# Moving the seven-product units of a feed-forward layer one place ahead among the up groups

## The chip, the cores and the metric

The kernel runs on one core of one Trainium2 chip. The metric is the device time of one execution in microseconds (us), the lower the better. Several executions were timed, and one more was recorded by the hardware profiler. Engines are called by their usual short names: PE is TensorE (matrix products), DVE is VectorE, ACT is ScalarE, POOL is GpSimd, SP is SyncE, which here only starts transfers.

## The reference

The program is a trunk of two encoder layers over 256 positions of width 2048, in float32. Each layer has a mixer (layer 0: pooling and attention, layer 1: a bidirectional mLSTM) and then a gated feed-forward block. Only the feed-forward block is touched by the change:

```python
D_MODEL, SEQ, D_FF, CONV_WIDTH = 2048, 256, 5632, 3

def conv_ffn(x, w_up, conv_w, conv_b, w_down):
    u = x @ w_up                                   # (256, 2048) @ (2048, 11264)
    up = jnp.pad(u, ((0, 0), (1, 1), (0, 0)))
    c = conv_w.astype(u.dtype)
    u = c[0] * up[:, :-2] + c[1] * up[:, 1:-1] + c[2] * up[:, 2:] + conv_b.astype(u.dtype)
    gate, val = jnp.split(u, 2, axis=-1)
    return (jax.nn.silu(gate) * val) @ w_down      # (256, 5632) @ (5632, 2048)

def reference(...):
    for layer in range(2):
        x = x + mixer(layer, rms_norm(x, norm_mix[layer]))
        x = x + conv_ffn(rms_norm(x, norm_ffn[layer]), w_up[layer], conv_w[layer], conv_b[layer], w_down[layer])
    return x
```

## The kernel before

Every float32 operand of a product is split into a high and a low part, and a product is made of three matrix products of the parts (high by high, high by low, low by high). Weights come from memory as tiles of 128 x 1024 numbers (512 KB). `Stream` loads them on SP's queue in the order in which PE will use them (`load`, up to five tiles ahead), and splits each (`split`): ACT makes the high part (L127) and DVE the low part (L128) of a tile called `hl`. Splits are written two tiles ahead of their use, and there are four `hl` buffers.

The inner width of 5632 is made of 44 row tiles of 128, in six chunks of 4, 8, 8, 8, 8 and 8 (`FCH`). For each row tile there is one **up group** (`up`, L980): 64 matrix products that take four weight tiles, and behind them a chain of small steps that makes the gated value. In order: ACT copies half of the sums (L427), DVE adds (L428) and scales (L984), six ACT steps make the convolution's three terms (L989 to L991), DVE adds them (L992, L993), ACT applies SiLU (L997), DVE multiplies gate by value (L998, tile `silu`, written `s` in the profile), and ACT (L999) and DVE (L1000) split that into the tile `g`.

The down projection is done in two ways. Some of it is a plain product (`down`, `down_two`; the last chunk and, in layer 0, half the columns of chunk 1; written `dn`). The rest takes two row tiles (a *pair* `j`) and 1024 columns (a *half* `h`) as a 2 x 2 matrix of blocks and multiplies with **seven block products in place of eight**. They are made in two passes, A with four products for each pair and B with three, since an A pass fills all four of PSUM's `ps` tiles (written `pp` in the profile). A piece of a pass in the order of work is a **unit** (`unit`, L1023): `("A", c, h, js)` is pass A of chunk `c`, half `h`, for the pairs `js`. A chunk of eight row tiles has four pairs, and a pass is two units, for pairs 0 and 1 and for pairs 2 and 3. Here a unit is written A c/h:js, such as A 3/1:01.

The products need sums of blocks on both sides:

- sums of the activations are made by `combine` (L1002, called a **mix**, one for each pair), out of the four `s` quarters of two row tiles: three DVE steps (L1006 to L1008) and then a split of the results by ACT (L1012) and DVE (L1013) into the tiles `s3` (384 wide, read by pass A) and `s1` (128 wide, read by pass B). Both are called `s` in the profile; the widths tell them apart;
- sums of the weights are, for half 1, made while they are loaded: a transfer with addition for one tile (`Sum`, started on POOL) and two DVE additions of half a tile each for the next (`Chain`, L123 and L124). For half 0 they were made long before by other transfers (`Made`).

When a pass is done, `drain` adds its PSUM tiles to `acc` or to `x` on DVE (L1068; the first time some by ACT). After the last unit of a half, `total` makes eight more DVE steps (L1085).

PE runs in the order in which the program is written. The order of the other engines is chosen when the program is built: of the steps that are ready there, the one written first. Which unit stands behind which up group is written out by `_ffn_plan` (L1232): behind each up group of chunk `c` it puts at most one place of work of chunk `c - 1`, counted from the first up group of chunk `c`. `_ffn_weights` lays out the weights in the same order. A mix stands behind the units of its place:

```python
        for i in range(n):
            seq.append(("up", c, i))
            seq += slots[i] if i < len(slots) else []
            if c < len(FCH) - 1:
                seq += [("mix", c, j) for j in range(n // 2) if i == max(2 * j + 1, busy.get(j, 0))]
```

The last up group of the second layer and of the first is number 43; behind it come its unit, then `down_two` (two blocks of 512 columns together, first with row tiles 0 to 5 of the last chunk, then with 6 and 7), and `down` for the other two blocks.

## Time and profile before

| what | value |
|---|---|
| median of 3 timed runs | 2163.98 us (2162.7 to 2164.5) |
| profiled execution: its own time, and the span from its first to its last instruction | 2163.78 us, 2162.0 us |
| PE busy with products, share of the span | 2156.2 us, 100% |
| DVE busy | 1734.7 us, 80% |
| ACT busy | 1414.3 us, 65% |
| POOL busy | 212.7 us, 10% |
| moved by transfers | 555.29 MB, mean 257 GB/s |

A row of the timeline gives the start in us from the span's start, the busy time, the engine, the line of the kernel, the operation, what is written and read (`out<-in`), the shape and the count; a bracket at its end gives the idle time of the engine before it and what ended that. In the table of waits, a row names who waited for whom, and then gives the us in total, the number of times and the longest wait. Granted clock is the share of full speed that PE was allowed.

### The profile page before, as it was taken

What the parts mean: (1) busy time and instruction counts of PE and PEld (TensorE: products, weight loads), DVE (VectorE), ACT (ScalarE), POOL (GpSimd) and SP (SyncE); (2) the same over time, 40 slices, a digit from 0 to 9 for tenths busy, and PEclk for the clock granted to TensorE, in tenths of its full rate; (3) what the DMA queues carried; (4) which work ended last, traced back from release to release, by engine and by line L of the source; (5) the groups of instructions that cost most, each with busy time, mean ns of one, the idle gap of its engine ahead of it and who ended that gap; (6) DMA issues with size and microseconds to landing.
All of it is one profiled execution on the core that took longest, in us unless ns stands there. A gap on an engine that the chain in (4) does not pass through costs nothing.

```text
span 2162.0 us, 31902 instructions
## 1 busy us (share of the span) xinstructions
PE 2156.2 (100%) x11412; PEld 1844.2 (85%) x11412; DVE 1734.7 (80%) x2425; ACT 1414.3 (65%) x2208; POOL 212.7 (10%) x268
## 2 busy tenths in 40 slices
PE   9999999999999999999999999999999999999999
PEld 7888888888888888889888888888888888888887
DVE  7686688887988988986777676667889898988896
ACT  7665578766777767666454544457777777776763
POOL 0022111110100100001111111211100000000000
PEclk9999999999999999999999999999999999999999
DMA  9668989898999877779888888898978787887774
GB/s 323 213 202 250 287 250 311 248 280 247 298 296 293 287 257 232 266 232 252 231 246 251 237 250 230 273 276 249 289 226 285 258 283 246 265 262 251 233 249 162
DMA packets 164097, 555.29 MB, mean 257 GB/s; under 512 B 20602, under 2 KB 23202, under 8 KB 163938
## 3 DMA queue, kind: packets, MB, share of 16 engines
q1 hardware_dynamic: 129632, 462.88, 62.0%
q0 software_dynamic: 20704, 52.71, 14.8%
q10 hardware_dynamic: 13602, 37.67, 5.7%
q8 instruction: 89, 1.46, 0.3%
q14 instruction: 70, 0.57, 0.1%
HBM read 551.04 MB, written 69.25 MB: 287 GB/s over the span
## 4 chain that ended last, share of the span: by engine, by line
PE 97%; DVE 2%; DMA 1%; issue 0%; ACT 0%; DVEq 0%
PE up L264 44%; PE pp L264 15%; PE op L264 8%; PE dn L264 5%; PE mv L264 4%; PE mq L264 4%; PE mk L264 4%; PE mo L264 4%; PE qproj L264 3%; PE kproj L264 1%; PE vproj L264 1%; PE pool L264 1%; DVE hl L128 1%; PE qk L264 1%; PE av L264 1%; PE end L264 1%
## 5 line engine op out<-in xcount | busy, mean ns | idle before, releaser
L128 DVE TENSOR_TENSOR hl<-w,hl 128x1024 fp32r<-128x1024 f32 (+2 forms) x840 | 1009.4, 1214 | 218.4 <-ACT hl L127 216.0
L127 ACT CAST hl<-w 128x1024 fp32r<-128x1024 f32 (+2 forms) x839 | 863.4, 1047 | 451.4 <-PE up L264 145.3
L264 PE MATMUL up<-xx,hl 128*128 128x512 f32 (+1 forms) x5632 | 994.0, 337 | 0.0
L264 PEld LDWEIGHTS up<-xx,hl 128*128 128x128 f32 x5632 | 866.9, 188 | 130.9 <-DVE hl L128 0.5
L264 PE MATMUL pp<-hl,s 128*128 128x512 f32 x816 | 204.9, 392 | 0.3 <-DVE hl L128 0.3
L264 PEld LDWEIGHTS pp<-hl,s 128*128 128x128 f32 x816 | 150.4, 188 | 32.0 <-DVE hl L128 1.2
L473 POOL DMA_DIRECT2D m<-m x128 | 102.1, 800 | 701.0 <-PE up L264 293.1
L264 PE MATMUL pp<-hl,g 128*128 128x512 f32 x612 | 156.9, 391 | 0.0
L427 ACT COPY tb_up<-up 128x512 f32<-128x512 f32 x88 | 51.6, 587 | 123.4 <-PE up L264 123.2
L264 PEld LDWEIGHTS pp<-hl,g 128*128 128x128 f32 x612 | 112.2, 188 | 22.3
L991 ACT ACTIVATE y<-tb_up,conv 128x256 f32<-128x256 f32 x176 | 104.4, 593 | 0.0
L992 DVE TENSOR_TENSOR y<-y,z 128x510 f32<-128x510 f32 x88 | 60.7, 689 | 52.2 <-ACT y L991 52.2
L473 POOL DMA_DIRECT2D m<-in_dn x64 | 54.6, 853 | 468.1 <-PE dn L264 168.1
L264 PE MATMUL dn<-hl,g 128*128 128x512 f32 x432 | 100.3, 391 | 0.0
L428 DVE TENSOR_TENSOR tb_up<-up,tb_up 128x512 f32<-128x512 f32 x88 | 60.8, 691 | 49.2 <-ACT tb_up L427 48.9
L264 PEld LDWEIGHTS dn<-hl,g 128*128 128x128 f32 x432 | 80.6, 188 | 16.6
L989 ACT ACTIVATE z<-tb_up,conv 128x256 f32<-128x256 f32 x176 | 88.9, 505 | 5.1 <-DVE tb_up L984 4.2
L264 PE MATMUL mk<-xx,hl 128*128 128x512 f32 (+1 forms) x512 | 92.2, 337 | 0.0
L264 PE MATMUL mq<-xx,hl 128*128 128x512 f32 (+1 forms) x512 | 92.1, 337 | 0.0
L264 PE MATMUL mv<-hl,xx 128*128 128x512 f32 (+2 forms) x480 | 91.7, 350 | 0.0
L264 PE MATMUL op<-hl,cat 128*128 128x512 f32 x384 | 91.6, 393 | 0.0
L264 PE MATMUL mo<-hl,xx 128*128 128x512 f32 x384 | 90.5, 391 | 0.0
(232 smaller groups left out, 2196.5 us busy)
## 6 DMA issues: line engine op xcount, KB each, us to landing
w<-in_up SPq DMA_DIRECT2D x352, 512.0 KB, 4.8
w<-in_dn SPq DMA_DIRECT2D x176, 512.0 KB, 4.6
w<-in_m_in SPq DMA_DIRECT2D x124, 512.0 KB, 5.1
m<-in_dn ACTq DMA_DIRECT2D x128, 256.0 KB, 5.5
w<-m SPq DMA_DIRECT2D x64, 512.0 KB, 5.0
w<-in_a_in SPq DMA_DIRECT2D x46, 512.0 KB, 5.3
sum<-in_dn SPq DMA_DIRECT2D x36, 512.0 KB, 5.4
sum<-in_dn POOLq DMA_DIRECT2D x36, 512.0 KB, 9.1
```

Of the source, the lines that this page charges most:

```text
L127: (self.nc.vector.tensor_copy if i + c == 0 else self.nc.scalar.copy)(hl[:, 0, c : c + n], w[:, c : c + n])
L128: low = self.nc.vector.tensor_sub(hl[:, 1, c : c + n], w[:, c : c + n], hl[:, 0, c : c + n].bitcast(F32))
L264: last_mm[0] = pe.matmul(out_, lhsT, rhs, start=start, stop=stop, skip_group_check=True)
L427: a.copy(tb, ps[:, :, 1, :])
L428: v.tensor_add(tb, ps[:, :, 0, :], tb)
L473: paced(eng.dma_start(to[p : p + P // 2], src[p : p + P // 2], **kw))
L989: a.activation(z[:, 0, j, :], u[:, j, :], AF.Copy, scale=cw(tl, 0))
L991: a.activation(y[:, j, :], u[:, j, :], AF.Identity, scale=cw(tl, 1), bias=cw(tl, 3))
L992: v.tensor_add(y[:, :, 1:S], y[:, :, 1:S], z[:, 0, :, 0 : S - 1])
```

## The change

`_ffn_plan` now keeps one list of 44 places for the whole layer. The units of a chunk of eight row tiles begin at the place of the chunk's own last row tile, where before they began at the place of the next chunk's first row tile. All units of such chunks stand one place further ahead; chunk 0, with two pairs, stays where it was. A mix stays with its own row tile, or, where it has to wait for an A unit that still reads the same `s3`, moves ahead with that unit. With the two orders side by side (number of the up group, then what stands behind it):

```
layer 1    before                              after
 26   B 2/0:01                            B 2/0:23
 27   B 2/0:23, mix 3/3                   A 3/1:01, mix 3/3
 28   A 3/1:01                            A 3/1:23
 29   A 3/1:23                            B 3/1:01
...
 42   B 4/0:01                            B 4/0:23
 43   B 4/0:23, two, down, down           two, two, down, down
```

Layer 0 is the same but in chunk 1, whose units are of one pair each: A 1/1:0 moves from behind group 12 to behind group 11, and mix 1/3 stays behind group 11, with A 1/1:3 three groups later. `down_two` is called in two parts that follow each other directly. Three small functions belong to a further possibility (`LAST`, a part of the last chunk by seven products) which is set to zero here: they give back what stood there before, for these numbers.

```diff
+LAST = (0, 0)
...
-                if kind == "B" and c == len(FCH) - 2:
+                if kind == "B" and c == _last_chunk(layer, h):
                     wv.add(total(h), 1.5)
...
-            def down_two(c):
+            def down_two(c, second):
 
                 gt, n = gts[c], FCH[c]
-                pss2 = [mmp.tile([P, 2, 512], F32, tag="mm", name=f"dn{layer}_{c}_{b}") for b in range(2)]
-                for kts in (range(n - 2), range(n - 2, n)):
-                    for ps in pss2:
-                        mov_part(ps, lambda k: gt[:, k], list(kts), kts[0] == 0, kts[-1] == n - 1)
+                if not second:
+                    twos.extend(mmp.tile([P, 2, 512], F32, tag="mm", name=f"dn{layer}_{c}_{b}") for b in range(2))
+                parts = [(ps, kts) for kts in (range(n - 2), range(n - 2, n)) for ps in twos]
+                for ps, kts in parts[1:] if second else parts[:1]:
+                    mov_part(ps, lambda k: gt[:, k], list(kts), kts[0] == 0, kts[-1] == n - 1)
+                if not second:
+                    return
...
+def _pairs(layer, c):
+
+    return (LAST[layer] if c == len(FCH) - 1 else FCH[c]) // 2
...
 def _ffn_plan(layer):
...
-    seq = []
+    slots = [[] for _ in range(FT)]
+    for c in range(len(FCH)):
+        pairs, halves = _pairs(layer, c), _halves(layer, c)
+
+        at = sum(FCH[: c + 1]) + (1 if pairs < 4 else -1)
+        if c == len(FCH) - 1:
+            at = FT - 1
+            ends = [(kind, c, 1, tuple(range(pairs))) for kind in "AB" if pairs]
+            slots[at] += ends[:1]
+        elif halves == (0, 1):
+            for h in (1, 0):
+                for kind in "AB":
+                    for js in ((0, 1), (2, 3))[: pairs // 2]:
+                        slots[at].append((kind, c, h, js))
+                        at += 1
+        else:
+            for k, kind in enumerate("AB"):
+                for j in range(pairs):
+                    slots[at + k * pairs + j].append((kind, c, 1, (j,)))
+            for b in range(2):
+                slots[at + (b + 1) * pairs // 2 - 1].append(("down", c, b))
+
+    busy = {(u[1], j): f for f, slot in enumerate(slots) for u in slot if u[0] == "A" for j in u[3]}
+    seq, f0 = [], 0
     for c, n in enumerate(FCH):
...
         for i in range(n):
             seq.append(("up", c, i))
-            seq += slots[i] if i < len(slots) else []
-            if c < len(FCH) - 1:
-                seq += [("mix", c, j) for j in range(n // 2) if i == max(2 * j + 1, busy.get(j, 0))]
-    return seq + [("two", len(FCH) - 1, 0)] + [("down", len(FCH) - 1, b) for b in range(2, NB)]
+            seq += slots[f0 + i]
+            seq += [("mix", c, j) for j in range(_pairs(layer, c))
+                    if i == max(2 * j + 1, busy.get((c - 1, j), 0) - f0)]
+        f0 += n
+    seq += [("two", c, 0)] + ends[1:] + [("two", c, 1)]
+    return seq + [("down", c, b) for b in range(2, NB)]
```

More of the change, by code (lines that the diff above doesn't have):

```diff
@@ L968, in ffn_layer @@
             acc = kp.tile([P, 2, 4, 512], F32, tag="acc", name=f"acc{layer}")
-            combos, pss, quads, seen = {}, {}, {}, set()
+            combos, pss, quads, seen, twos = {}, {}, {}, set(), []
             conv = kp.tile([P, NC_CONV], F32, tag="conv", name=f"conv{layer}")
@@ L1023, in unit @@
             def unit(kind, c, h, js):
-                n = FCH[c] // 2
+                n = _pairs(layer, c)
                 order = (4, 6, 5, 3) if kind == "A" else (0, 1, 2)
@@ L1118, in down @@
                 gt, last = gts[c], c == len(FCH) - 1
-                kts = list(range(FCH[c]))
+                kts = list(range(_direct(layer, c, b), FCH[c]))
                 if last and nxt is None and b == NB - 1:
@@ L1131, in down @@
                     nxt.add(b)
-            def down_two(c):
+            def down_two(c, second):
                 gt, n = gts[c], FCH[c]
-                pss2 = [mmp.tile([P, 2, 512], F32, tag="mm", name=f"dn{layer}_{c}_{b}") for b in range(2)]
-                for kts in (range(n - 2), range(n - 2, n)):
-                    for ps in pss2:
-                        mov_part(ps, lambda k: gt[:, k], list(kts), kts[0] == 0, kts[-1] == n - 1)
+                if not second:
[5 more added lines that the diff above has]
+                    return
                 wv.until(lambda: ("A", 0) not in seen or ("total", 0) in pss)
-                for b, ps in enumerate(pss2):
+                for b, ps in enumerate(twos):
                     residual(ps, b)
@@ L1160, in ffn_layer @@
                 elif kind == "two":
-                    down_two(c)
+                    down_two(c, i)
                 elif kind == "mix":
@@ L1227, in _halves @@
 def _halves(layer, c):
-    return () if c in (-1, len(FCH) - 1) else (0, 1) if c in BOTH[layer] else (1,)
-def _ffn_plan(layer):
-    seq = []
-    for c, n in enumerate(FCH):
-        pairs = FCH[c - 1] // 2 if c else 0
-        halves = _halves(layer, c - 1)
-        if halves == (0, 1):
-            slots = [[(kind, c - 1, h, js)] for h in (1, 0) for kind in "AB"
-                     for js in ((0, 1), (2, 3))[: pairs // 2]]
-            slots = [[]] * (pairs < 4) + slots
-        else:
-            slots = [[(kind, c - 1, 1, (j,))] for kind in "AB" for j in range(pairs)]
-            for b in range(2 if pairs else 0):
-                slots[(b + 1) * pairs // 2 - 1].append(("down", c - 1, b))
-        busy = {j: k for k, slot in enumerate(slots) for u in slot if u[0] == "A" for j in u[3]}
+    return () if c == len(FCH) - 1 else (0, 1) if c in BOTH[layer] else (1,)
@@ new lines, in _pairs, with _last_chunk, _direct @@
+def _pairs(layer, c):
+    return (LAST[layer] if c == len(FCH) - 1 else FCH[c]) // 2
+def _last_chunk(layer, h):
+    return len(FCH) - (1 if h and LAST[layer] else 2)
+def _direct(layer, c, b):
+    return LAST[layer] if c == len(FCH) - 1 and b >= NB // 2 else 0
+def _ffn_plan(layer):
+    slots = [[] for _ in range(FT)]
[20 more added lines that the diff above has]
+    seq, f0 = [], 0
+    for c, n in enumerate(FCH):
@@ L1266, in _down_chunks @@
         rows = w[k0 * P : (k0 + n) * P]
-        blocks = [_mov(rows[:, b * 512 : b * 512 + 512]) for b in range(NB) if b // 2 not in _halves(layer, c)]
+        blocks = [_mov(rows[_direct(layer, c, b) * P :, b * 512 : b * 512 + 512]) for b in range(NB) if b // 2 not in _halves(layer, c)]
         if c == len(FCH) - 1:
@@ L1272, in _down_chunks @@
         k0 += n
-    n = sum(FCH[:-1]) // 2
+    n = (sum(FCH[:-1]) + LAST[layer]) // 2
     res = [np.concatenate(out)]
@@ L1294, in _ffn_weights @@
         elif kind in ("down", "two"):
-            out += [next(down) for _ in range(FCH[c] // 2 * (2 if kind == "two" else 1))]
+            n = FCH[c] // 2 - 1
+            out += [next(down) for _ in range((n, n + 2)[i] if kind == "two" else (FCH[c] - _direct(layer, c, i)) // 2)]
         elif kind != "mix":
```

## The prediction

> **What bounds the kernel now.** I read the page's busy times and its slices first, then who PE waited for, then the timeline around the last row tile of one chunk.

> ```profile
> PE 2156.2 (100%) x11412; PEld 1844.2 (85%) x11412; DVE 1734.7 (80%) x2425; ACT 1414.3 (65%) x2208; POOL 212.7 (10%) x268
> ...
> PEclk9999999999999999999999999999999999999999
> ```

> PE is busy for 2156.2 of 2162.0 us and its clock is granted in full in every slice. A busy PE could still be a waiting one, so the table of what PE waited for comes next; its first two rows are the longest of four:

> ```profile
> PE wps L288 <- DVE pad L682: 1.2, 1, 1.2
> PE pp L264 <- DVE hl L128: 0.3, 1, 0.3
> ```

> So PE is the bound from end to end. The feed-forward stages hold almost no wait that a better order could take away: 1.2 us is the start of the program, and the one wait in a unit is 0.3 us. The change alters no matrix product, no weight tile and no transfer, only their order. Its gain can therefore be about 1 us at most; its loss is whatever PE has to wait in the new order. What matters is how early each operand is ready now, against when PE will ask for it. The timeline of PE around up group 27 of layer 1, the last row tile of chunk 3 (start, duration):

> ```profile
> 1855.20 2.89 PE L264 MATMUL pp<-hl,g 128*128 128x512 f32 x12
> ...
> 1859.31 11.30 PE L264 MATMUL up<-xx,hl 128*128 128x512 f32 x64
> 1870.44 2.24 PE L264 MATMUL pp<-hl,s 128*128 128x512 f32 x9
> ...
> 1875.97 11.30 PE L264 MATMUL up<-xx,hl 128*128 128x512 f32 x64
> 1887.11 2.24 PE L264 MATMUL pp<-hl,s 128*128 128x512 f32 x9
> ...
> 1889.88 2.22 PE L264 MATMUL pp<-hl,s 128*128 128x512 f32 x9
> ```

> Group 27 ends at 1855.20. Unit B 2/0:23 follows (4.1 us, to 1859.31), then group 28 (11.13 us), unit A 3/1:01 from 1870.44 (5.53 us), group 29, and A 3/1:23 from 1887.11. That unit makes four products with pair 2 and then, at 1889.88, begins those with pair 3, which read the `s3` of mix 3/3. From the end of group 27 to that point are 34.7 us.

> And DVE's side of the same row tile, from the adding of the sums of group 27 to the end of mix 3/3:

> ```profile
> 1856.02 0.69 DVE L428 TENSOR_TENSOR tb_up<-up,tb_up 128x512 f32<-128x512 f32 x1 [0.76 <-ACT tb_up L427]
> ...
> 1869.09 0.42 DVE L998 TENSOR_TENSOR s<-s,y 128x256 f32<-128x256 f32 x1
> ...
> 1871.17 0.42 DVE L1006 TENSOR_TENSOR sf<-s 128x256 f32<-128x256 f32 x1
> ...
> 1873.66 0.28 DVE L1007 TENSOR_TENSOR sf<-sf,s 128x128 f32<-128x128 f32 x1
> ...
> 1878.68 0.55 DVE L1013 TENSOR_TENSOR s<-sf,s 128x384 fp32r<-128x384 f32 x1
> ```

> SiLU times value (L998) is done 14.3 us behind the group's end (1869.51 less 1855.20), the 384-wide `s3` 24.0 us behind it (1879.23 less 1855.20). Now that leaves 10.7 us of the 34.7. The 9.7 us from the one to the other hold 1.2 us of DVE work of the mix (0.42, 0.28 and 0.55); the rest is waiting in turn between splits. A row of the windows says how full DVE is behind the group's end:

> ```profile
> 1855.20:1874.60 19.40, 19.40 (x103) 16.50 (x102) 18.57 (x27) 14.21 (x20) 0.85 (x1) 1.00 0.66 222
> ```

> DVE works 18.57 of these 19.40 us, so each step of the chain queues behind a 1.2 us split or two.

> **The change part by part.**

> *The time that mix c/3 has.* In the new order A 3/1:01 follows group 27 at once, then group 28, then A 3/1:23. That is the stretch which now runs from 1870.44 (end of group 28) to 1889.88: PE will ask for the new `s3` 19.4 us behind group 27, where it now asks 34.7 us behind. At today's 24.0 us it would be 4.6 us late, and nothing else is there for PE to do meanwhile, since its order is fixed. The queue behind the waiting product holds all of PE; behind that stand the `hl` splits that need a buffer PE has not freed, and the loads behind them.

> *Where it happens.* At every chunk of eight whose first unit now stands right behind its last row tile, with pairs 2 and 3 one group later: chunks 2, 3 and 4 of layer 0 and chunks 1 to 4 of layer 1, seven places. Chunk 0 stands still. Chunk 1 of layer 0 goes by single pairs, and asks for its pair 3 three groups behind its last row tile, over 33 us: no wait.

> *How late.* What DVE does in those 19.4 us changes in both directions, so 24.0 can't simply be kept. From below: the same chain at group 7 of layer 0, right behind which A 0/0:01 stands already, with ready-made weights and so without the four half-tile additions of `Chain`:

> ```profile
> 357.08 2.24 PE L264 MATMUL pp<-hl,s 128*128 128x512 f32 x9
> ```
> ```profile
> 368.24 0.42 DVE L998 TENSOR_TENSOR s<-s,y 128x256 f32<-128x256 f32 x1
> ...
> 373.66 0.55 DVE L1013 TENSOR_TENSOR s<-sf,s 128x384 fp32r<-128x384 f32 x1
> ```

> There `s3` is done 17.1 us behind the group's end at 357.08 (5.6 us after L998), in time by 2.3 us: the lower end is no wait. From above: group 28 now has just such a unit of half 1 behind it, with the `Chain` additions, and its L998 comes later than group 27's:

> ```profile
> 1886.90 0.42 DVE L998 TENSOR_TENSOR s<-s,y 128x256 f32<-128x256 f32 x1
> ...
> 1891.76 0.42 DVE L1000 TENSOR_TENSOR g<-s,g 128x256 fp32r<-128x256 f32 x1
> ```

> 16.9 us behind 1870.44, or 2.6 more. With the 9.7 us of mix 3/3 on top `s3` comes after 26.6 us, 7.2 us late: the upper end. I take a value between. Group 28's L998 shares its window with the steps of mix 3/3 (1.25 us in the three rows above), which in the new order come behind it, so 15.6 us. With the 5.6 us of group 7 that gives 21.2, with the 9.7 us of group 27 it gives 25.3; the middle is 23.2, near the 24.0 that the same tile has today. That is 3.8 us late at six places, 22.8 us.

> *Layer 1, chunk 1* has two free places ahead of it (groups 9 and 10), so DVE comes to it with less behind it:

> ```profile
> 1615.19 2.24 PE L264 MATMUL pp<-hl,s 128*128 128x512 f32 x9
> ```
> ```profile
> 1623.88 0.55 DVE L1013 TENSOR_TENSOR s<-sf,s 128x384 fp32r<-128x384 f32 x1
> ```

> Group 11 ends one up group (11.14 us) ahead of 1615.19, at 1604.05; `s3` is done 20.4 us later. I take 1.0 us late; bounds as above, 0 to 7.2.

> *The end of a layer.* The row tile 43 loses the unit behind it: `down_two` reads its `g` (row tile 7) after 2 x 36 matrix products of row tiles 0 to 5 and 6 of row tile 6, at 0.228 us (144 in 32.80 us) 17.8 us behind the group's end, where it now has 21.9 us.

> ```profile
> 2110.46 2.89 PE L264 MATMUL pp<-hl,g 128*128 128x512 f32 x12
> ...
> 2114.56 32.80 PE L264 MATMUL dn<-hl,g 128*128 128x512 f32 x144
> ```
> ```profile
> 2125.76 0.42 DVE L1000 TENSOR_TENSOR g<-s,g 128x256 fp32r<-128x256 f32 x1
> ```

> `g` is done 15.7 us behind 2110.46: cost nothing, covered by 2 us. If the cover goes, because `drain` and `total` of half 0 now fall into this window, the 21.7 us of `g` at group 28 (1892.18 less 1870.44) is the far end: 3.9 us in each layer. I take 0.

> *The rest* goes by order alone and is costed at nothing. Each pass still has an up group behind it in which its PSUM tiles are drained. The transfers with addition keep their distance to the units that use them, since units, groups and loads all move together; SP and POOL are moved past nothing new but at the two ends of the row of units. `s1`, `s3` and the two `g` buffers come free earlier, not later. `total` of half 0 ends earlier, under group 43, where nobody waited for it.

> *Sum:* 22.8 + 1.0 = 23.8 us on the profiled execution's 2163.8 us (1.8 us above its span, and 0.2 us under the median of the runs): 2187.6, say 2188 us. That case alone reaches from six places at 1.8 us (21.2) with none at the seventh, 2175 us, to six at 5.9 (25.3) with 3 at the seventh, 2202 us.

> **The rivals.** Less than 0.2% (4.3 us) is about what a measurement of this kernel can't tell from no change.

> *In time after all (not slower).* The order of DVE is made anew, and mix c/3 is now written ahead of group c+1,0, so its steps may go ahead of most splits. It decides at 19.4 us: with `s3` as at group 7 (17.1 us) every place is free and the time stays at 2164 us, within 1 us. For it: the mix needs only 1.2 us of DVE, and PE's need of splits in the stretch leaves DVE some slack. Against: the four `Chain` additions, and the two places above that have them near are at 20.4 and 24.0 us today. Chance 0.19.

> *The clock falls.* No wait in this trace is long enough to show what PE's clock does after one; it is granted in full throughout. If each wait of 3.8 us were followed by as long a time at half clock, 1.9 us more would be lost at each of seven places: 13 us, 2201 us. Against it: such a wait would come once in eight up groups, and may come out shorter. Chance 0.08. [...]

> *Late only at the end of the layers.* Mixes in time but `g` of row tile 43 late: up to 8 us, 2168 to 2172 us. Chance 0.04.

> *Much later* than the upper end, by splits and loads that fall behind at each stop: above 2205 us, chance 0.05. *Faster* by over 4.3 us would need waits that PE doesn't have: 0.02.

> **How the numbers follow.** The forecast's own case has 0.62. Slower: 0.62 + 0.08 + 0.04 + 0.05 = 0.79, less 0.01 for a forecast case under 4.3 us, 0.78. Same: 0.19 + 0.01 = 0.20. Faster: 0.02. Without the case of no change under 8 in 10 would be held, so the range begins at 2163 us; it ends at 2205 us, above the forecast's 2202 and the clock's 2201.

> **What would show it.** In the changed profile PE should wait, at seven places, in a unit A c/1:23 for DVE's `s` (L1013), some 19 us behind the last row tile of the chunk, for 1.8 to 5.9 us each; the stretches between stay back to back, with 11.1 us for an up group. Up groups slower than that behind a wait show the clock. No PE wait for `s` and the same span show the first rival. The prediction is wrong if DVE's new order puts L1006, L1007 and L1013 right behind L998, or if PE waits for something else, such as `hl` or a transfer.

## The result

The changed kernel takes 2187.25 us (median of 5 runs, 2184.93 to 2190.21), the kernel before 2163.47 us (5 runs, 2162.7 to 2164.5): a ratio of 1.011, 95% interval 1.0095 to 1.0125. It is slower, by 23.8 us, and 2188 us was forecast. In the profile after, lines stand one further down than before (the split on DVE is L129, ACT's half of a mix L1013, DVE's L1014); in the runs below they shift by a few more, and the tiles' names tell the rows apart.

The profiled execution took 2186.75 us, its span 2185.0 us. The page's first line and what PE waited for, to be read against those of before:

```profile
PE 2163.4 (99%) x11412; PEld 1846.7 (85%) x11412; DVE 1739.5 (80%) x2425; ACT 1413.3 (65%) x2208; POOL 210.4 (10%) x268
```
```profile
PE pp L265 <- DVE s L1014: 9.5, 6, 1.8
PE pp L265 <- ACT s L1013: 6.6, 7, 4.8
PE wps L289 <- DVE pad L683: 1.2, 1, 1.2
```

Two rows are new: PE waits in seven units for the mix's `s`, 16.1 us in all. PE at one of these places, unit A 3/1:23 of layer 1, and DVE ahead of it:

```profile
1877.57 2.24 PE L265 MATMUL pp<-hl,s 128*128 128x512 f32 x9
...
1896.32 0.86 PE L265 MATMUL pp<-hl,g 128*128 128x512 f32 x3
1897.38 0.73 PE L265 MATMUL pp<-hl,s 128*128 128x512 f32 x2 [0.21 <-ACT s L1013]
1899.70 1.88 PE L265 MATMUL pp<-hl,s 128*128 128x512 f32 x7 [1.58 <-DVE s L1014]
```
```profile
1892.15 0.42 DVE L999 TENSOR_TENSOR s<-s,y 128x256 f32<-128x256 f32 x1
1892.73 1.22 DVE L129 TENSOR_TENSOR hl<-sum,hl 128x1024 fp32r<-128x1024 f32 x1 [0.16 <-ACT hl L128]
1893.88 0.42 DVE L1007 TENSOR_TENSOR sf<-s 128x256 f32<-128x256 f32 x1
...
1895.67 0.28 DVE L1008 TENSOR_TENSOR sf<-sf,s 128x128 f32<-128x128 f32 x1
1896.01 1.23 DVE L129 TENSOR_TENSOR hl<-w,hl 128x1024 fp32r<-128x1024 f32 x1
...
1897.95 1.22 DVE L129 TENSOR_TENSOR hl<-w,hl 128x1024 fp32r<-128x1024 f32 x1
1899.09 0.55 DVE L1014 TENSOR_TENSOR s<-sf,s 128x384 fp32r<-128x384 f32 x1
```

Up group 27 ends at 1877.57. L999 (L998 before) is done 15.0 us later, `s3` 22.1 us later (1899.64), and its reader could have begun after 19.4. Two products go ahead once ACT's high half is there; the third stands still for DVE's low half. Against PE's usual spacing (5.5 us for such a unit, 11.14 us for an up group) this place loses 2.3 us, and chunk 4 of layer 0 and chunks 2 and 4 of layer 1 lose the same; chunk 1 of layer 1 loses 2.1. Chunks 2 and 3 of layer 0 lose more, 7.7 and 4.7 us (the first two rows are of chunk 2, the others of chunk 3):

```profile
560.08 0.86 PE L265 MATMUL pp<-hl,g 128*128 128x512 f32 x3
565.71 4.31 PE L265 MATMUL pp<-hl,s 128*128 128x512 f32 x9 [4.77 <-ACT s L1013]
...
697.25 0.73 PE L265 MATMUL pp<-hl,s 128*128 128x512 f32 x2 [0.75 <-ACT s L1013]
699.77 2.24 PE L265 MATMUL pp<-hl,s 128*128 128x512 f32 x7 [1.80 <-DVE s L1014]
```

In chunk 2 the wait is longer (4.77 us) and ended by ACT's half, and the nine products behind it take 4.31 us, where the nine at 1877.57 take 2.24. The windows say why. A row gives the stretch and its length, the busy time and count of PE, PE's weight loads, DVE, ACT and POOL, then the granted clock, the busy share of the transfers and GB/s:

```profile
561.00:564.50 3.50, 0.00 (x0) 0.00 (x0) 3.50 (x6) 3.45 (x7) 0.00 (x0) 1.00 1.03 420
564.60:571.40 6.80, 5.69 (x13) 4.31 (x14) 5.21 (x10) 3.16 (x8) 1.68 (x2) 0.50 1.03 302
571.50:575.00 3.50, 3.50 (x22) 3.06 (x21) 2.60 (x4) 1.65 (x2) 0.79 (x1) 1.00 1.03 249
...
701.20:704.50 3.30, 3.30 (x10) 2.62 (x10) 3.27 (x5) 2.37 (x3) 1.68 (x2) 0.50 0.97 236
...
1895.00:1905.00 10.00, 8.21 (x39) 6.27 (x38) 9.69 (x15) 8.41 (x15) 1.69 (x2) 1.00 0.91 274
```

PE's clock is at half behind the waits of these two places, and full around a regular one. The seven losses are 7.7 + 4.7 + 2.3 in layer 0 and 2.1 + 3 x 2.3 in layer 1, 23.9 us with the decimals kept; 0.9 us that PE lost at 573 and 701 us of the kernel before are gone, which gives the 23.0 us between the spans.

### The profile page after: what moved, and what is told of

The parts are those of the page before. It is cut to its first block, busy times and chain, and to the rows that moved or that the text cites. A ratio compares the mean times of both kernels' runs of the same rounds, so it can differ in the third digit from the quotient of the medians.

```text
span 2185.0 us, 31916 instructions
## 1 busy us (share of the span) xinstructions
PE 2163.4 (99%) x11412; PEld 1846.7 (85%) x11412; DVE 1739.5 (80%) x2425; ACT 1413.3 (65%) x2208; POOL 210.4 (10%) x268
## 4 chain that ended last, share of the span: by engine, by line
PE 95%; DVE 2%; DMA 2%; issue 1%; ACT 0%; ACTq 0%; DVEq 0%; POOLq 0%
PE up L265 43%; PE pp L265 14%; PE op L265 8%; PE dn L265 4%; PE mv L265 4%; PE mq L265 4%; PE mk L265 4%; PE mo L265 4%; PE qproj L265 3%; DMA sum<-in_dn 1%; DVE hl L129 1%; PE kproj L265 1%; PE vproj L265 1%; PE qk L265 1%; PE av L265 1%
## 5 line engine op out<-in xcount | busy, mean ns | idle before, releaser
L129 DVE TENSOR_TENSOR hl<-w,hl 128x1024 fp32r<-128x1024 f32 (+2 forms) x840 | 1009.0, 1214 | 237.5 <-ACT hl L128 234.7
L128 ACT CAST hl<-w 128x1024 fp32r<-128x1024 f32 (+2 forms) x839 | 861.1, 1045 | 483.0 <-PE up L265 158.0
L265 PE MATMUL pp<-hl,s 128*128 128x512 f32 x816 | 209.1, 397 | 16.1 <-DVE s L1014 9.5
L428 ACT COPY tb_up<-up 128x512 f32<-128x512 f32 x88 | 51.5, 585 | 117.8 <-PE up L265 117.6
L993 DVE TENSOR_TENSOR y<-y,z 128x510 f32<-128x510 f32 x88 | 60.6, 689 | 53.1 <-ACT y L992 53.0
L265 PE MATMUL op<-hl,mcat 128*128 128x512 f32 x384 | 89.5, 392 | 0.0
```

Source lines behind the costliest of these rows:

```text
L128: (self.nc.vector.tensor_copy if i + c == 0 else self.nc.scalar.copy)(hl[:, 0, c : c + n], w[:, c : c + n])
L129: low = self.nc.vector.tensor_sub(hl[:, 1, c : c + n], w[:, c : c + n], hl[:, 0, c : c + n].bitcast(F32))
L265: last_mm[0] = pe.matmul(out_, lhsT, rhs, start=start, stop=stop, skip_group_check=True)
L428: a.copy(tb, ps[:, :, 1, :])
L993: v.tensor_add(y[:, :, 1:S], y[:, :, 1:S], z[:, 0, :, 0 : S - 1])
```

## The experiments

**One layer alone.** The places of layer 0 stay as before:

```diff
-        at = sum(FCH[: c + 1]) + (1 if pairs < 4 else -1)
+        at = sum(FCH[: c + 1]) + (1 if pairs < 4 else -layer)
```

> Only layer 1 has the new places, layer 0 keeps the old ones. If each place costs what the trace after shows there (2.1 us at chunk 1, 2.34 us at chunks 2 to 4 of layer 1), 9.2 us on top of before: about 2172.6 us. If the loss belongs to layer 0, with its transfers, or to something that all moved units share, 2164 to 2166 us.

Measured: 2175.28 us against 2163.57, ratio 1.0052 (1.0039 to 1.0065), 11.7 us. Layer 1 shows the four losses of the trace after to the tenth, 9.2 us together. The rest is layer 0, which has its old places and yet 2.1 us more of small waits than in the trace of before; those that PE's table lists are for splits (the longest 0.86 us). Why these came is open. The loss is not layer 0's alone: each moved chunk pays its own.

**The load beside the mix.** The weight sums of half 1 are left out:

```diff
-                    out += [Sum(s0[q], s1[q]), Chain(r[q])]
+                    out += [s0[q], r[q]]
```

> The new order, but the weight sums of half 1 are left out (plain weights are loaded, with no transfer with addition and none of the half-tile additions L123 and L124 of the kernel before). If the load of DVE in the 19.4 us behind the last row tile makes the mix late, s3 comes as it does at group 7 of the kernel before, 17 to 18 us behind the group's end, and no wait is left: 2163 to 2165 us. If the chain of the mix is late whatever DVE has beside it, about 2180 us, with only the two long waits shortened.

Measured: 2162.87 us, ratio 0.9997 (0.9987 to 1.0006). PE waits in no unit any more. DVE and PE at the same place, group 27 of layer 1:

```profile
1874.69 0.75 DVE L1014 TENSOR_TENSOR s<-sf,s 128x384 fp32r<-128x384 f32 x2
```
```profile
1858.34 2.24 PE L265 MATMUL pp<-hl,s 128*128 128x512 f32 x9
```

`s3` (the row holds both writes) is begun 16.35 us behind the group's end and, at the 0.55 us of its write, done after 16.9, where it took 22.1. The chain is the same; gone are DVE's additions beside it and the transfers with addition that feed them, and this run doesn't tell the two apart. With `s3` in time, the new order costs nothing, and gains nothing that can be measured: a PE that is never idle has nothing to give.

**The order beside the mix.** Splits that PE doesn't need yet are held until `s3` is written:

```diff
+            high = (self.nc.vector.tensor_copy if i + c == 0 else self.nc.scalar.copy)(hl[:, 0, c : c + n], w[:, c : c + n])
...
+            if i in self.held:
+                for mine, other in zip((high, low), self.held[i]):
+                    self.behind(mine, other)
...
-                    a.copy(d[:, 0], e)
-                    v.tensor_sub(d[:, 1], e, d[:, 0].bitcast(F32))
+                    both = a.copy(d[:, 0], e), v.tensor_sub(d[:, 1], e, d[:, 0].bitcast(F32))
+                    if j == 3 and d is s3 and _halves(layer, c) == (0, 1):
+                        st.held.update({st.at + 7 + n: both for n in range(3)})
```

> The new order, but with the splits of the three weight tiles behind the one that meets the late s3 (the last tile of unit A c/1:23 and two of the next up group) held back on ACT and DVE until mix c/3 has written s3, at the six places of whole units. If the waits come from the order on DVE (two splits of 1.14 us stand between the mix's steps), s3 comes some 2 us earlier: the regular waits of 2.3 us fall to 0 to 0.5 us, chunk 3 of layer 0 loses its clock fall too, and the time is about 2173 us, with chunk 2 of layer 0 still late behind its transfer. If DVE simply has too much work in those 19.4 us, PE waits for the held splits in place of s3 and the time stays at 2185 to 2188 us.

The edit holds them at all seven places, on ACT and on DVE. Measured: 2172.43 us, ratio 1.0043 (1.0031 to 1.0056): 14.8 of the 23.8 us are back. DVE and PE at group 27 of layer 1, which ends at 1867.42:

```profile
1885.52 0.28 DVE L1012 TENSOR_TENSOR sf<-sf,s 128x128 f32<-128x128 f32 x1
1885.72 0.69 DVE L989 TENSOR_TENSOR tb_up<-tb_up,R 128x512 f32<-128x512 f32 x1
1886.32 0.28 DVE L1013 TENSOR_TENSOR sf<-sf,s 128x128 f32<-128x128 f32 x1
1886.52 0.55 DVE L1017 TENSOR_TENSOR s<-sf,s 128x384 fp32r<-128x384 f32 x1
1887.33 3.50 DVE L130 TENSOR_TENSOR hl<-w,hl 128x1024 fp32r<-128x1024 f32 x3 [0.26 <-ACT hl L129]
```
```profile
1867.42 2.24 PE L269 MATMUL pp<-hl,s 128*128 128x512 f32 x9
...
1886.86 2.48 PE L269 MATMUL pp<-hl,s 128*128 128x512 f32 x9
```

The three splits now stand behind `s3`, which is done after 19.6 us; the nine products take 2.48 us in place of 2.24, a loss under 0.3 us. At the regular places the wait was order, and DVE had room for all its work. Chunk 3 of layer 0 falls from 4.7 to 1.2 us. Chunk 2 keeps 7.3 us.

**Chunk 2 of layer 0: the transfers.** In the trace after, DVE stood idle there for a transfer with addition, and the convolution of the late row tile (L993) was queued behind it:

```profile
553.62 0.69 DVE L124 TENSOR_TENSOR w<-w,sum 128x512 f32<-128x512 f32 x1 [2.28 <-DMA sum<-in_dn]
554.23 0.68 DVE L993 TENSOR_TENSOR y<-y,z 128x510 f32<-128x510 f32 x1
```

Two runs lighten the transfers. The first takes away those that make layer 0's other weight sums at the time:

```diff
         for i, e in enumerate(mixes[layer]):
+            if layer == 0:
+                e[3][0].ap, e[3][1].ap = e[0], e[2]
+                continue
```

> The new order, but layer 0's weight sums for half 0 are not made by transfers beforehand (plain weights are loaded in their place, so that the sums are left out); 14 of the 32 sets of such transfers go. If the two long waits, of chunks 2 and 3 of layer 0, and the fall of the clock behind them come from transfers that crowd those of the weight sums of half 1, they fall to the regular 2.3 us: 8.0 to 2.3 and 4.7 to 2.3, so 2187.2 less 8.1, about 2179 us. If they come from the mix alone, 2187 us.

Measured: 2183.18 us, ratio 1.009 (1.0076 to 1.0104). The two places fall only from 7.7 and 4.7 to 6.0 and 4.2 us, and at chunk 2 the granted clock falls again (0.72 as the mean from 564 to 570 us): a miss, between the two cases expected. The second takes away the addition itself in chunks 2 and 3:

```diff
-                    out += [Sum(s0[q], s1[q]), Chain(r[q])]
+                    out += [Sum(s0[q], None if layer == 0 and c in (2, 3) else s1[q]), Chain(r[q])]
```

> The new order, but in chunks 2 and 3 of layer 0 the weight sums of half 1 are loaded without the transfer that adds the second part (so that part of the sum is left out; the loads, the half-tile additions on DVE and every step of PE stay). In the trace after, DVE's addition L124 stood 2.3 us idle for that transfer behind group 19, with the convolution of the late row tile queued behind it. If that is what makes the waits of chunks 2 and 3 of layer 0 long, they fall to the regular 2.3 us and the clock stays full there: 7.7 and 4.7 to 2.3 each, 2187.2 less 7.8, about 2179 us. If not, 2185 to 2187 us.

Measured: 2184.65 us, ratio 1.0096 (1.0078 to 1.0114): near the case in which that transfer does not make the waits long. DVE no longer stands idle for it, but chunk 2 still loses 5.8 us. Of the 1.9 us that it gains, 0.6 is a shorter wait (4.18 us), and most of the rest is faster products behind it (the twelve of the wait's unit take 4.42 us in place of 5.59). ACT shows what is left:

```profile
561.00 1.05 ACT L129 CAST hl<-w 128x1024 fp32r<-128x1024 f32 x1
561.95 0.51 ACT L991 ACTIVATE z<-tb_up,conv 128x256 f32<-128x256 f32 x1
...
564.05 0.59 ACT L993 ACTIVATE y<-tb_up,conv 128x256 f32<-128x256 f32 x1
564.54 0.70 ACT L1014 CAST s<-sf 128x384 fp32r<-128x384 f32 x2
```

ACT makes all six convolution steps of the next up group before its half of `s3`. At the regular place of the trace after it makes them behind it (L1013 at 1896.83, the first step at 1898.21). **The order on ACT** was tried together with the held splits; the six steps wait there for ACT's half of `s3`:

```diff
...
+                        if i == 0 and st.c3 and st.c3[1] == c:
+                            behind(step, st.c3[0])
...
```

> As the run with splits held behind s3, and besides the six convolution steps of the next up group (L989 to L991 of the kernel before) are held on ACT behind ACT's half of s3. In chunk 2 of layer 0 four of them ran ahead of it. If that wait too is one of order, on ACT, s3 comes 1.6 us earlier there, the wait falls from 3.3 us to under 2 us and the clock stays full: 2172.4 less 1.6 and less some 2.4 us of half clock, about 2168 us. If it comes from the late transfer alone, 2171 to 2173 us.

Measured: 2172.51 us, ratio 1.0043 (1.0029 to 1.0056), no better than the splits alone. The wait for `s` in chunk 2 does fall, from 3.0 to 1.7 us, but the held splits are late in its place:

```profile
PE pp L269 <- ACT hl L129: 1.9, 1, 1.9
PE pp L269 <- ACT s L1019: 1.7, 1, 1.7
PE wps L293 <- DVE pad L687: 1.2, 1, 1.2
PE pp L269 <- DVE hl L130: 1.0, 1, 1.0
```

And both orders with the lighter loads:

> Both holds on the order (splits and convolution steps behind s3) together with the lighter loads of chunks 2 and 3 of layer 0 (the transfer that adds the second part is left out there, and so that part of the sum). Each alone left chunk 2 of layer 0 with 7.1 and 5.8 us. If that place is late by both, the transfer that DVE stands idle for and the order on ACT and DVE, its wait now falls to 0.5 to 1.5 us with the clock full, and the whole kernel comes to 2165 to 2167 us. If a third cause holds it, 5 us or more stay there and the time is 2170 us or more.

Measured: 2170.89 us, ratio 1.0033 (1.002 to 1.0045): the second case expected, a third cause. The wait for `s` is down to 0.6 us, so the lateness of `s3` in chunk 2 is made by the transfer and the order together. But the 1.9 and 1.0 us for the held split remain, with slower products behind them (three take 1.27 us, where three ahead of the waits take 0.86), 6.2 us in all. The third cause is thus the hold itself: it helps at the other six places and costs at this one. A version with a shorter hold there wasn't tried, so it is open whether chunk 2 can be freed of its whole loss by order and transfer.

**The clock.** Steps are put into mix c/3 to make `s3` later by design (5 in place of 2 in the second run):

```diff
+                for _ in range(2 if j == 3 else 0):
+                    v.tensor_scalar_mul(sf[:, 0:3], sf[:, 0:3], 1.0)
```

> The new order with two more DVE steps (a 384-wide product with 1.0, one behind the other) in mix c/3 of each chunk of eight, so that s3 comes later by design. One step takes some 0.5 us, and with a split in between up to 1.7, so s3 comes 1 to 3.4 us later at seven places, and PE's waits grow from 2.3 to between 3.3 and 5.7 us. If each us of lateness costs a us and nothing else, 2194 to 2211 us. If PE's clock falls to half behind a wait of more than about 2.5 us (it did behind those of 2.6 and 5 us, and not behind those of 2.3 us), some 2.5 us more at each of the five places where it has not so far: 2207 to 2224 us, with the granted clock near 0.5 behind every wait.

> The same with five more steps: 2.5 to 8.5 us later at seven places, though DVE has less beside the chain once PE stands still. By waits alone 2205 to 2247 us; with the clock's fall behind each, 2217 to 2260 us. Against the run with two more steps, three more at seven places: if the clock's loss does not grow with the wait's length, the difference is the waits' alone.

Measured: 2213.55 us, ratio 1.0228 (1.0214 to 1.0242), and 2229.63 us, ratio 1.0304 (1.029 to 1.0318). The waits for `s`, of the run with two steps and the run with five:

```profile
PE pp L265 <- ACT s L1015: 36.0, 7, 7.6
```
```profile
PE pp L265 <- ACT s L1015: 50.1, 7, 8.3
```

In the two profiled executions, two steps add 19.9 us of waits to the 16.1, but 27.3 us to the span (2212.3 us against 2185.0); three more add 14.1 of waits and 14.4 to the span (2226.7 us). The mean granted clock is 0.992 and 0.989, where it was 0.998 in the trace after. At chunk 1 of layer 1 with two steps, and at chunk 3 with five, it is at half, and full again in the last row:

```profile
1650.20:1653.50 3.30, 3.17 (x8) 2.45 (x9) 2.23 (x5) 1.10 (x4) 0.85 (x1) 0.50 0.94 235
```
```profile
1929.90:1936.60 6.70, 4.13 (x10) 3.27 (x11) 3.25 (x9) 2.28 (x4) 0.00 (x0) 0.50 1.04 276
1936.80:1942.00 5.20, 5.20 (x30) 4.50 (x29) 4.54 (x6) 2.11 (x2) 0.00 (x0) 1.00 0.48 146
```

Against the span before (2162.0 us) they are 50.3 and 64.7 us longer; less the waits listed that is 2.0 and 2.1 us for each of the seven places (0.55 us at a regular place of the trace after, at full clock). The mean wait grew from 5.1 to 7.2 us, and this extra time did not grow with it.

## Why the prediction was right, point by point

The sum was right: 23.8 us forecast, 23.8 measured. The mechanism was right too: seven places, the reader of mix c/3's `s3`, 19.4 us, nothing else waiting. That the late `s3` is the whole loss is shown by the trace after, where PE waits in the units for nothing else and the seven losses add up to the difference, and by the run that made it early (2162.87 us). The terms were sized less well, and errors cancelled: four places were 1.5 us too dear each, the other three 3.9, 0.9 and 1.1 us too cheap. That the total agrees to the tenth is luck.

*Six places at 3.8 us* were 2.3 us at four of them. The step that failed is the middle between 21.2 and 25.3: L998 came after 15.0 us (15.6 were taken), and from there `s3` took 7.1 us (5.6 to 9.7 were the ends). So it was 2.7 us late, not 3.8; the lower reading was nearer. Of the 2.7 us PE lost 2.3. What I had not seen is that PE needs ACT's half first, so that two products run while DVE writes the other.

*Chunk 1 of layer 1 at 1.0 us* was 2.1. Its 20.4 us were measured with no unit right behind group 11; with one there it is no better off than the others.

*Chunks 2 and 3 of layer 0* were counted with the regular ones and lost 7.7 and 4.7 us. "The transfers with addition keep their distance", at no cost, is one step that failed for chunk 2, worth at most 1.9 of the 7.7 us; the order on ACT, which the prediction had no term for, is another. The trace of before had said that this place has less room, in rows that I did not use:

```profile
567.74 0.55 DVE L1013 TENSOR_TENSOR s<-sf,s 128x384 fp32r<-128x384 f32 x1
```
```profile
539.39 1.53 PE L264 MATMUL pp<-hl,g 128*128 128x512 f32 x6
...
572.01 1.78 PE L264 MATMUL pp<-hl,s 128*128 128x512 f32 x7
```

That is the same mix of chunk 2, done 28.9 us behind its group's end at 539.39 and 3.7 us ahead of its reader at 572.01; chunk 3 of layer 1 had 10.7 us to spare. For chunk 3 of layer 0 the trace of before gave no such sign: its `s3` took 24.1 us there, as at the regular places. It lost 2.4 us more than these, 0.8 by longer waits and 1.6 by the clock.

*The rival of the clock* was held at 0.08 as a thing of all seven places. It came at two, those with the longest waits (granted 0.50 for 6.83 us at chunk 2 and 3.41 us at chunk 3), and was worth about 2.4 us at chunk 2 (7.7 less the regular 2.3, less 3.0 us of longer waits) and 1.6 at chunk 3. The price taken for it, 1.9 us a place, was about right. At chunk 3 the waits ahead of it were 0.75 and 1.80 us.

*In time after all* was wrong for the first reason given against it: with the additions and their transfers gone it is exactly what happens.

*The end of the layers* cost nothing, as said: PE has no wait in `dn`.

## What to carry to other kernels

Where one engine is busy for 100% of the span, an order that brings work forward has next to nothing to gain, and its price is read from the slack of each operand: the time from its making to its first use, in the old order, less what the new order takes away. That is an estimate, since the new order also changes what else the engines do in that time: by it a regular place would be 4.6 us late, and was 2.7. Take the slack place by place; a row that is late but harmless today (28.9 us against 17 to 24) is the first to hurt. A chain of short steps on a full engine is made late by the long steps put between its links: holding those back won 14.8 us, with all the work kept, where lighter transfers in layer 0 won 2.6 and 4.1 us.

## What the runs showed of the hardware

```profile
561.17:564.58 3.41, 0.00 (x0) 0.00 (x0) 3.41 (x6) 3.36 (x7) 0.02 (x1) 1.00 1.03 420
564.59:568.00 3.41, 2.29 (x5) 1.65 (x6) 2.87 (x7) 1.70 (x5) 1.10 (x2) 0.50 1.00 351
568.00:571.41 3.41, 3.41 (x9) 2.67 (x9) 2.36 (x4) 1.48 (x3) 0.59 (x1) 0.50 1.05 255
571.42:701.11 129.69, 127.14 (x676) 108.11 (x676) 111.78 (x146) 90.74 (x138) 11.95 (x15) 1.00 0.88 281
...
697.71:701.12 3.41, 1.61 (x8) 1.13 (x7) 3.41 (x7) 3.29 (x9) 0.85 (x1) 1.00 1.05 396
701.12:704.53 3.41, 3.41 (x11) 2.73 (x10) 3.38 (x5) 2.44 (x3) 1.68 (x2) 0.50 0.95 231
704.54:2170.00 1465.46, 1456.71 (x7757) 1247.18 (x7756) 1182.02 (x1619) 936.67 (x1392) 116.03 (x148) 1.00 0.81 250
```

PE is idle (the length less its busy time) for all of the piece ahead of the first stretch, and for 1.80 us of the piece ahead of the second. With 1.12 us of idle time at half clock (from 564.59 us) half clock went on; with none (from 568.00 and from 701.12 us) full clock followed. At the regular places the clock stayed full. Two pieces of the same trace, counted on from these, at chunk 1 of layer 1 and at the regular place shown above:

```profile
1636.37:1639.78 3.41, 1.82 (x8) 0.86 (x6) 3.41 (x5) 3.41 (x7) 0.85 (x1) 1.00 1.07 358
...
1895.79:1899.20 3.41, 2.12 (x8) 1.07 (x7) 3.35 (x6) 3.41 (x7) 0.84 (x1) 1.00 0.91 351
```

PE is idle for 1.59 us of the first and 1.29 us of the second. The regular place has waits of 0.21 and 1.58 us, 1.79 us together, but the second of them reaches into the next piece. In the run with less to add, chunk 3 of layer 0 has the same sum in 0.75 and 1.04 us, and there the clock falls:

```profile
695.36 0.73 PE L266 MATMUL pp<-hl,s 128*128 128x512 f32 x2 [0.75 <-ACT s L1014]
697.13 2.78 PE L266 MATMUL pp<-hl,s 128*128 128x512 f32 x7 [1.04 <-DVE s L1015]
```
```profile
697.90:701.20 3.30, 3.30 (x9) 2.51 (x8) 2.65 (x5) 2.52 (x6) 0.88 (x2) 0.50 1.00 230
```

So the same sum of waits had half clock behind it at one place and full clock at another. That the idle time within one such piece makes the difference, and that the regular places kept the clock partly by chance, is my reading of these rows; no run tested it.
